# A three-mixer trunk on one core: the scan's decay work ordered behind its group's values, group sums in four column tiles, running sums by zero-padded products

## The chip, the cores and the metric

The kernel runs on one core of a Trainium2 chip. The metric is the device time of one execution in microseconds (us), and lower is better. Three timed runs of the kernel before gave 811.83, 812.42 and 811.11 us, median 811.83. The profile is that of a further execution, which took 812.16 us.

Engine names in the profile: PE is TensorE's matrix products and PEld its weight loads; DVE is VectorE, ACT is ScalarE, POOL is GpSimd, SP is SyncE. A name with q (ACTq) is an engine's queue issuing a DMA. L829 is line 829 of the kernel before.

## What is computed

Two residual layers on 256 tokens of 1024 channels, and a final norm. In each layer one wide projection of the normalised stream feeds three causal mixers (a state-space scan in the Mamba-2 manner, sliding-window attention, forgetting attention). Each mixer's output is projected back, weighted by a sigmoid gate, and the sum goes through an output projection. Cut to what the change touches:

```python
def ssd_chunked_scan(xh, dt, a, bm, cm):        # chunks of 128 tokens, 4 groups of 4 heads
    x_dt = x * dtc[..., None]
    a_cum = jnp.cumsum(dtc * a, axis=-1)          # running sum inside a chunk
    seg = a_cum[..., :, None] - a_cum[..., None, :]
    decay = jnp.where(causal, jnp.exp(jnp.where(causal, seg, 0.0)), 0.0)
    y_diag = einsum(cb[:, :, None] * decay, x_dt)
    decay_states = jnp.exp(a_cum[..., -1:] - a_cum)
    states = einsum(bc, decay_states, x_dt)
    ...
def grouped_rms_norm(y, w, groups):               # 4 groups of 256 channels
    y = y * rsqrt(mean(y * y over the group) + EPS)
    ...
def forgetting_attention_branch(...):
    cum = cumsum(log_sigmoid(f_logit + f_bias))   # over all 256 tokens
    scores + cum[query] - cum[key], causal softmax, times values
```

## The kernel before

**Weights and products.** Weights stream through `raw` tiles by SyncE's DMAs. ScalarE rounds each to a high half `hi` (L293), VectorE takes the low half `lo` as the difference (L294), and TensorE multiplies with both (fast float32r products, the records `mm<-hi`, `mm<-lo`). The activations are split in the same way. Small products (scores, values, transposes, the ones here) are plain float32 and write to PSUM tiles `mx`.

**Order of the work.** TensorE's order is written out by a planner while the program is built. `clock["t"]` counts the planned TensorE time (`mm` and `transpose`, L103 to L113, add a cost each). The dense products run in a fixed list. Every side job is a generator that yields a delay; `pump()` and `drain()` place its next stage between dense products when the planned clock has passed that delay. On TensorE that order is kept. On VectorE, ScalarE and GpSimd the scheduler of the tile framework picks an order that it deems ready first, and the built program then issues each engine's instructions strictly in that order. `tc.issue_after(x)` orders what is issued in its block behind `x`. `T("L1", ...)` takes a tile from a rotating set of buffers of that size.

**The decay logits** (`decay_logits`, L765 to L811). VectorE computes the steps `dt` and the log forget values `lf` for both chunks of 128 tokens, and writes `rates` (tokens on partitions; chunk, kind, 16 heads). After `D_CUM` TensorE makes the running sums: `tri` times the scan's rates gives tokens by heads (L799, kept as `acum`); `rates` as weights against `tri` give heads by tokens, 32 rows for each chunk (L801); a third product with `ones` adds the first chunk's total to the second chunk's forget sums (L803). ScalarE copies the 64 rows out and writes them to `cumd` in DRAM (L807 to L811), so that they can be read back by DMA as broadcasts over all partitions.

**The scan** (`ssd_group`, L852 to L915; four groups in each layer). A group fetches its broadcast `bcg` from `cumd` (L858, issued by ScalarE's queue), yields, transposes its inputs on TensorE (L867) and evicts them times `dt` into `xdt` (L868, VectorE). Then come `ds` (last running sum less the token's own, 128x4, L871), its exponential (L872, ScalarE), `xds = xdt * ds` (L874), eight subtractions with the causal mask (L881), the exponentials of the two decays (L883) and of `cross` (L887). A stage later two products C times B are made (L893, L894) and multiplied into the decays (L896), and a stage after that TensorE makes the outputs (L901 to L910) and VectorE adds the skip term (L913).

**Others in the same stretch.** The convolution of the scan's inputs runs three taps on VectorE (L829), a tanh on ScalarE (L835) and a product on VectorE (L836). Sliding-window attention transposes its probabilities on TensorE; ScalarE copies the first half (L676), VectorE masks the second half with `other` (L678) and with `tri` (L679); the products with values of two quads of heads follow (L711, the batches `mx<-L,bias` and `mm<-L,bias`). Forgetting attention loads a bias per pair of heads (L1050), masks it on GpSimd (L1057) and uses it on VectorE (L649).

**Group norm of the scan's output** (`group_norms`, L959 to L978). For each of four groups and each half of the tokens, the 128x128 tile of squares is the weights and two columns of `ones` are the moving operand (L966): the sums land with tokens on partitions. VectorE scales (L968), GpSimd raises to the power -1/2 (L969), VectorE makes one Newton step (L973 to L975). `u_proj_normed` uses the roots at its evictions (L1000, L1002).

Of the kernel before, what the change touches and what calls it, by code (L numbers as in the profile page):

```python
# [13 lines left out]
AF = mybir.ActivationFunctionType  # L14
ALU = mybir.AluOpType

P = 128
S = 256
# [4 lines left out]
EPS = 1e-6  # L23

D_SOFT, D_SOFT2, D_EVAC, D_SSD, D_SSD2 = 7.0, 3.0, 3.0, 8.0, 4.0
D_K, D_Q, D_QK, D_G0, D_FOX, D_BDMA, D_BIAS, D_BC, D_SSD3 = 6.0, 5.5, 2.0, 8.0, 0.0, 4.0, 2.6, 5.5, 1.0
D_GN1, D_GN2, D_CUM, D_H, D_M = 8.0, 13.5, 17.0, (4.8, 6.4), 5.0
BUDGET = 1.35
T_PP, T_SSD, T_BIAS = 1, 1, 1
D_MEET = 12.0  # L30
# [20 lines left out]
def hybrid_trunk(  # L51
# [5 lines left out]
    nc = tc.nc  # L57
# [45 lines left out]
    def mm(o, a, b, **kw):  # L103
        n = b.free_size()
        if a.dtype == F32R:
            clock["t"] += max(0.094, n / 2350.0)
        else:
            clock["t"] += max(0.2, n / 587.0) * (0.5 if a.free_size() == 64 or a.shape[0] == 32 else 1.0)
        nc.tensor.matmul(o, a, b, **kw)  # L109

    def transpose(o, a, i):
        clock["t"] += 0.109
        nc.tensor.transpose(o, a, i)  # L113
# [76 lines left out]
    ident = T("ident", [P, P])  # L190
    make_identity(nc, ident)
    tri = T("tri", [P, P])
# [3 lines left out]
    negtri = T("negtri", [P, P])  # L196
# [7 lines left out]
    ones = onesr.bitcast(F32)  # L204
# [223 lines left out]
    for l in range(L):  # L428
        y = Layer()
# [335 lines left out]
    def decay_logits(y):  # L765
        u = y.u

        tmp = T("L1", [P, 4, 2, 32])
        e = w = tmp[:, 0, :, :]
        act(e, u, AF.Abs)  # L770
        act(e, e, AF.Exp, scale=-1.0)
        s = tmp[:, 1, :, :]
        ts(s, e, 2.0, None, op0=ALU.add)
        nc.vector.reciprocal(s, s)
        tt(s, s, e, op=ALU.mult)
        s2 = tmp[:, 2, :, :]
        tt(s2, s, s, op=ALU.mult)
        q = tmp[:, 3, :, :].rearrange("p t c -> p (t c)")
        s2f = s2.rearrange("p t c -> p (t c)")
        sf = s.rearrange("p t c -> p (t c)")  # L780
        ts(q, s2f, 1.0 / 19.0, None, op0=ALU.mult)
        for m in (17, 15, 13, 11, 9, 7, 5, 3):
            stt(q, q, 1.0 / m, s2f, op0=ALU.add, op1=ALU.mult)
        stt(q, q, 1.0, sf, op0=ALU.add, op1=ALU.mult)
        q3 = q.rearrange("p (t c) -> p t c", t=2)
        y.dt = T("dt", [P, 2, 16])
        rates = T("rates", [P, 2, 2, 16])
        lf = tmp[:, 2, :, 0:16]
        ts(w[:, :, 0:16], u[:, :, 0:16], 0.0, 0.5, op0=ALU.max, op1=ALU.mult)
        tt(y.dt, w[:, :, 0:16], q3[:, :, 0:16], op=ALU.add)  # L790
        ts(y.dt, y.dt, 2.0, None, op0=ALU.mult)
        ts(w[:, :, 16:32], u[:, :, 16:32], 0.0, 0.5, op0=ALU.min, op1=ALU.mult)
        tt(lf, w[:, :, 16:32], q3[:, :, 16:32], op=ALU.subtract)
        ts(rates[:, :, 0, :], lf, -16.0, None, op0=ALU.mult)
        tt(rates[:, :, 1, :], y.dt, bc(y.nega, 1, 2), op=ALU.mult)
        yield D_CUM

        pc = pmx()
        mm(pc[:, P:P + 32], tri, rates[:, :, 1, :], start=True, stop=True)  # L799
        for c in range(2):  # L800
            mm(pc[32 - 32 * c:64 - 32 * c, 0:P], rates[:, c, :, :].rearrange("p w c -> p (w c)"), tri,  # L801
               start=True, stop=(c == 0))
        mm(pc[0:16, 0:P], rates[:, 0, 0, :], ones, start=False, stop=True)  # L803
        y.acum = T("acum", [P, 2, 16])
        act(y.acum, pc[:, P:P + 32].rearrange("p (t c) -> p t c", t=2), AF.Copy)
        cum = T("L1", [64, P])
        act(cum, pc[0:64, 0:P], AF.Copy)  # L807
        y.cumd = dr.tile([2, 16, S], F32, name=f"cumd{y.l}", tag=f"cumd{y.l}")
        for c in range(2):
            nc.scalar.dma_start(y.cumd[:, :, c * P:(c + 1) * P].rearrange("w c s -> (w c) s"),  # L810
                                cum[32 - 32 * c:64 - 32 * c, :])  # L811


    def u_conv(y, u, c):
# [37 lines left out]
    def ssd_group(y, g):  # L852
        yield lambda: not any(m[2] == 1 for m in waiting)
        if g == 0:
            yield D_SCAN
        yield "bcg"
        bcg = T("L4", [P, 4, S])
        nc.scalar.dma_start(bcg, y.cumd[1, 4 * g:4 * g + 4, :].partition_broadcast(P))  # L858
        yield D_BC
        yield "ssd"  # L860
        xdt = T("L2", [P, 2, 256])
        hs = slice(4 * g, 4 * g + 4)
        p = pmx()
        for t in range(2):
            for j in range(2):
                n = 2 * t + j
                transpose(p[:, n * P:(n + 1) * P], y.xs[:, 2 * g + j, t * P:(t + 1) * P], ident)  # L867
        tt(xdt.rearrange("p t (h d) -> p t h d", h=4), p.rearrange("p (t h d) -> p t h d", t=2, h=4),  # L868
           bc(y.dt[:, :, hs], 3, 64), op=ALU.mult)
        ds = T("ds", [P, 4], bufs=2)  # L870
        tt(ds, bcg[:, :, P - 1], y.acum[:, 0, hs], op=ALU.subtract)  # L871
        act(ds, ds, AF.Exp)  # L872
        xds = T("L1", [P, 256])
        tt(xds.rearrange("p (h d) -> p h d", h=4), xdt[:, 0, :].rearrange("p (h d) -> p h d", h=4),  # L874
           bc(ds, 2, 64), op=ALU.mult)
        decs = []
        for c in range(2):
            tk = slice(c * P, (c + 1) * P)
            dec = T("L2", [P, 4, P])
            for h in range(4):  # L880
                stt(dec[:, h, :], bcg[:, h, tk], y.acum[:, c, 4 * g + h:4 * g + h + 1], negtri,  # L881
                    op0=ALU.subtract, op1=ALU.add)
            act(dec, dec, AF.Exp)  # L883
            decs.append(dec)

        cross = T("L2", [P, 4, P])
        act(cross, bcg[:, :, P:S], AF.Exp)  # L887
        decs.append(cross)
        yield D_SSD
        tokens["bcg"] += 1  # L890

        p = pmx()
        mm(p[:, 0:S], y.bcT[:, g, 0:P], y.bcT[:, 4 + g, :], start=True, stop=True)  # L893
        mm(p[:, S:3 * P], y.bcT[:, g, P:S], y.bcT[:, 4 + g, P:S], start=True, stop=True)  # L894
        for dec, c in zip(decs, (0, 2, 1)):
            tt(dec, dec, bc(p[:, c * P:(c + 1) * P], 1, 4), op=ALU.mult)  # L896
# [62 lines left out]
    def group_norms(y, squares):  # L959


        p = pmx()
        for g, q in enumerate(squares):
            for t in range(2):
                c = 4 * g + 2 * t
                mm(p[:, c:c + 2], q[:, t * P:(t + 1) * P], ones[:, 0:2], start=True, stop=True)  # L966
        v, r0 = T("sm", [P, 8]), T("sm", [P, 8])
        ts(v, p[:, 0:16].rearrange("p (g i) -> p g i", i=2)[:, :, 0], 1.0 / 256, 4 * EPS, op0=ALU.mult, op1=ALU.add)  # L968
        gtt(r0, v, mhalf, op=ALU.pow)  # L969

        def newton():
            y.roots = T("rs", [P, 8], bufs=4)
            tt(v, r0, v, op=ALU.mult)  # L973
# [431 lines left out]
    with tc.manual_schedule(engines={ENG.PE, ENG.DVE, ENG.Activation, ENG.Pool}):  # L1405
# [11 lines left out]
        p = pmx()  # L1417
# [151 lines left out]
```

## Time and profile before

| what | us |
|---|---|
| median of three timed runs | 811.83 |
| the profiled execution | 812.16 |
| its span in the trace | 810.5 |
| PE busy, all | 799.6 |
| PE busy between 100 and 200 us | 98.63 |
| PE busy between 500 and 600 us | 98.49 |
| DVE busy between 200 and 300 us | 93.08 |

The times on the left of timelines and chain pieces are us from the start of the span. Layer 1 fills about the first half of it and layer 2 the second, with the same stages about 398 us later. "Busy" of PE is the union of its product records. A product in float32 shows as two records, a fast one or a transpose as one. A bracket at the end of a timeline row says how long the engine had been idle and what released it. In a row of a group the numbers after the bar are the total busy time and the mean ns of one record.

### The profile page before, as it was taken

To read this page: it belongs to the slowest core of one execution; us is meant where nothing else is said; L and a number is where in the kernel's file an instruction comes from. 1 tells how busy PE (TensorE), PEld (TensorE's weight loads), DVE (VectorE), ACT (ScalarE), POOL (GpSimd) and SP (SyncE) were. 2 spreads that over 40 slices of the span, in tenths; PEclk is the share of its full clock that TensorE was granted. 3 is DMA by queue.
4 is the path that set the end of the run, shared out by engine and by line. 5 is a ranking of instruction groups with operands and counts; after the bars stand their busy time and mean duration, and the time that the engine had idled before them with its cause. 6 is when DMAs were issued, how large, how long until landed. Compare 5 with 4: busy or idle time off the path is not lost.

```text
span 810.5 us, 14858 instructions
## 1 busy us (share of the span) xinstructions
PE 799.6 (99%) x5178; PEld 714.4 (88%) x5178; DVE 684.6 (84%) x1412; ACT 532.7 (66%) x1142; POOL 167.8 (21%) x236
## 2 busy tenths in 40 slices
PE   9999999999999999999999999999999999999996
PEld 8998988888888888888999899887889988888896
DVE  6878999898898998795785889998979999869865
ACT  7777768775775785543665588676747768745452
POOL 3066113130321000033001831122312110002000
PEclk9999999999999999999999999999999999999999
DMA  9997887697665565676678987679986646567632
GB/s 314 277 265 178 245 228 202 185 291 230 174 210 159 165 189 179 211 248 209 221 249 259 247 204 213 153 216 257 280 226 185 201 143 186 175 226 218 211 107 75
DMA packets 138826, 170.43 MB, mean 210 GB/s; under 512 B 9352, under 2 KB 106464, under 8 KB 138752
## 3 DMA queue, kind: packets, MB, share of 16 engines
q1 hardware_dynamic: 114960, 140.53, 55.1%
q0 software_dynamic: 13328, 13.29, 10.2%
q10 hardware_dynamic: 10464, 15.67, 6.4%
q8 instruction: 41, 0.67, 0.3%
q14 instruction: 33, 0.27, 0.1%
HBM read 154.71 MB, written 2.16 MB: 194 GB/s over the span
## 4 chain that ended last, share of the span: by engine, by line
PE 97%; DMA 1%; DVE 1%; ACT 0%; issue 0%; POOL 0%; ACTq 0%; POOLq 0%
PE mm L109 83%; PE mx L109 10%; PE mx L113 4%; DMA L<-cumd 1%; DVE lo L294 0%; DVE L L678 0%; ACT L L293 0%; DVE L L836 0%; DVE L L1431 0%; DVE L L1088 0%; ACT L L1435 0%; ACT L L1212 0%; DVE L L829 0%; DVE L L1187 0%; DVE L L1191 0%
## 5 line engine op out<-in xcount | busy, mean ns | idle before, releaser
L109 PE MATMUL mm<-L,hi 128*128 128x512 f32 x1056 | 354.0, 387 | 0.2
L294 DVE TENSOR_TENSOR lo<-raw,hi 128x1024 fp32r<-128x1024 f32 (+1 forms) x276 | 313.1, 1154 | 38.8 <-ACT hi L293 36.0
L109 PE MATMUL mm<-hi,L 128*128 128x512 f32 (+2 forms) x1168 | 303.1, 349 | 0.1
L293 ACT ACTIVATE hi<-raw 128x1024 fp32r<-128x1024 f32 (+1 forms) x276 | 266.1, 983 | 55.9 <-PE mm L109 49.0
L109 PE MATMUL mm<-L,lo 128*128 128x256 f32 x1056 | 266.6, 273 | 0.0
L109 PEld LDWEIGHTS mm<-hi,L 128*128 128x128 f32 x1168 | 205.9, 190 | 22.4 <-issue 1.0
L109 PEld LDWEIGHTS mm<-L,hi 128*128 128x128 f32 x1056 | 194.9, 190 | 27.2 <-issue 5.4
L109 PEld LDWEIGHTS mm<-L,lo 128*128 128x128 f32 x1056 | 202.1, 191 | 5.4
L109 PE MATMUL mm<-lo,L 128*128 128x512 f32 (+2 forms) x584 | 201.5, 347 | 0.0
L109 PEld LDWEIGHTS mm<-lo,L 128*128 128x128 f32 x584 | 110.2, 190 | 10.8 <-DVE lo L294 0.2
L491 POOL DMA_DIRECT2D L<-L x68 | 59.5, 895 | 194.0 <-ACT L L490 131.2
L829 DVE SCALAR_TENSOR_TENSOR L<-L,vec,L 128x255 f32<-128x255 f32 (+2 forms) x96 | 46.3, 482 | 1.8
L1057 POOL TENSOR_SCALAR_AFFINE_SELECT bias<-bias 128x128 f32<-128x128 f32 x64 | 32.1, 535 | 74.7 <-DMA bias<-cumd 70.9
L489 ACT ACTIVATE L<-mm 128x256 f32<-128x256 f32 x84 | 31.9, 380 | 19.5 <-PE mm L109 15.5
L655 ACT ACTIVATE pp<-pp,nm 128x128 f32<-128x128 f32 x64 | 28.2, 442 | 23.8 <-DVE nm L649 23.8
L1091 ACT ACTIVATE L<-L 128x512 f32<-128x512 f32 x24 | 15.1, 631 | 39.3 <-DVE L L1088 34.7
L491 POOL DMA_DIRECT2D qt<-L x16 | 13.8, 859 | 78.7 <-ACT qt L490 71.8
L1088 DVE TENSOR_TENSOR L<-mm,L 128x512 f32<-128x512 f32 x22 | 15.1, 688 | 16.5 <-PE mm L109 8.8
L613 ACT ACTIVATE pp<-pp,nm 128x128 f32<-128x128 f32 x32 | 12.6, 394 | 24.7 <-DVE nm L618 23.9
L835 ACT ACTIVATE L<-L 128x256 f32<-128x256 f32 x32 | 13.4, 418 | 22.2 <-DVE L L829 22.1
L490 ACT ACTIVATE L<-mm 128x256 f32<-128x256 f32 x68 | 26.2, 385 | 1.8 <-DMA L<-L 1.8
L1124 POOL TENSOR_TENSOR L<-L,L 128x512 f32<-128x512 f32 x8 | 11.9, 1491 | 71.3 <-DVE L L1123 69.9
(211 smaller groups left out, 920.0 us busy)
## 6 DMA issues: line engine op xcount, KB each, us to landing
raw<-in_w_in_dram SPq DMA_DIRECT2D x191, 512.0 KB, 5.0
raw<-in_w_proj_dram SPq DMA_DIRECT2D x48, 512.0 KB, 6.1
L<-L POOLq DMA_DIRECT2D x72, 128.0 KB, 5.3
raw<-in_w_out_dram SPq DMA_DIRECT2D x16, 512.0 KB, 5.6
bias<-cumd ACTq DMA_DIRECT2D x16, 256.0 KB, 3.5
L<-cumd ACTq DMA_DIRECT2D x8, 512.0 KB, 7.0
L<-in_gate_bias_dram ACTq DMA_DIRECT2D x12, 256.0 KB, 5.9
qt<-L POOLq DMA_DIRECT2D x16, 128.0 KB, 5.9
```

The source lines that it names most:

```text
L109: nc.tensor.matmul(o, a, b, **kw)
L113: nc.tensor.transpose(o, a, i)
L293: keep(act)(hi, src, AF.Copy)
L294: keep(tt)(lo, src, hi.bitcast(F32), op=ALU.subtract)
L489: act(halves(lo), ordered(p[:, S:2 * S]), AF.Copy)
L490: last = act(halves(out), ordered(p[:, 0:S]), AF.Copy)
L491: nc.gpsimd.dma_start(out, lo, accum_op=ALU.add)
L655: act(pp[:, i, sl], pp[:, i, sl], AF.Exp, scale=-1.0, bias=nm[:, e:e + 1], accum_out=sums[:, e:e + 1])
L829: stt(a[:, s:S], x_[:, 0:S - s], y.vec[:, 16 * j + u:16 * j + u + 1], a[:, s:S], op0=ALU.mult, op1=ALU.add)
L1057: nc.gpsimd.affine_select(out=bias[:, i, dst], in_=bias[:, i, src], compare_op=ALU.is_ge, fill=NEG, base=0, pattern=[[-1, P]], channel_mul ...
L1088: tt(halves(g), p, halves(y.gb), op=ALU.add)
L1091: finish(act(g, g, AF.Tanh, scale=0.5))
```

## The change

Three edits, and a constant that goes with the second (`D_GN2`, which the kernel before defines and doesn't use).

1. In `ssd_group` the `ds` work, `xds` and the decays are built inside `tc.issue_after(own.ins)`, where `own` is the eviction into `xdt`; `cross` is built behind the exponential of the second decay.
2. In `group_norms` the roles of weights and moving operand are exchanged: 32 columns of `ones` are the weights, a group's 128x256 squares move, and group g writes PSUM rows 32g to 32g+31 (each of these rows holds the same sums). ScalarE copies the 128x256 sums out, after `D_GN2` = 3.0 of planned time TensorE transposes them in two halves, and VectorE picks one column of 32 from each group.
3. In `decay_logits` the rates are written into the first columns of a zeroed 128x128 tile `all_`, and the first chunk's forget rates once more into a zeroed tile `past`, at the columns of the second chunk's forget rates. Two products of full width, accumulated, give all 64 rows; the order of the two chunks' rows is exchanged. GpSimd zeroes both tiles by one memset.

```diff
-D_GN1, D_GN2, D_CUM, D_H, D_M = 8.0, 13.5, 17.0, (4.8, 6.4), 5.0
+D_GN1, D_GN2, D_CUM, D_H, D_M = 8.0, 3.0, 17.0, (4.8, 6.4), 5.0
...
-        rates = T("rates", [P, 2, 2, 16])
+        wide = T("L1", [P, 2, P])
+        nc.gpsimd.memset(wide, 0.0)
+        all_, past = wide[:, 0, :], wide[:, 1, :]
+        rates = all_[:, 0:64].rearrange("p (t w c) -> p t w c", t=2, w=2)
...
+        ts(past[:, 32:48], lf[:, 0, :], -16.0, None, op0=ALU.mult)
         yield D_CUM
 
         pc = pmx()
+        mm(pc[:, 0:P], all_, tri, start=True, stop=False)
+        mm(pc[:, 0:P], past, ones, start=False, stop=True)
         mm(pc[:, P:P + 32], tri, rates[:, :, 1, :], start=True, stop=True)
-        for c in range(2):
-            mm(pc[32 - 32 * c:64 - 32 * c, 0:P], rates[:, c, :, :].rearrange("p w c -> p (w c)"), tri,
-               start=True, stop=(c == 0))
-        mm(pc[0:16, 0:P], rates[:, 0, 0, :], ones, start=False, stop=True)
...
-                                cum[32 - 32 * c:64 - 32 * c, :])
+                                cum[32 * c:32 + 32 * c, :])
...
-        tt(xdt.rearrange("p t (h d) -> p t h d", h=4), p.rearrange("p (t h d) -> p t h d", t=2, h=4),
-           bc(y.dt[:, :, hs], 3, 64), op=ALU.mult)
-        ds = T("ds", [P, 4], bufs=2)
-        tt(ds, bcg[:, :, P - 1], y.acum[:, 0, hs], op=ALU.subtract)
-        act(ds, ds, AF.Exp)
+        own = tt(xdt.rearrange("p t (h d) -> p t h d", h=4), p.rearrange("p (t h d) -> p t h d", t=2, h=4),
+                 bc(y.dt[:, :, hs], 3, 64), op=ALU.mult)
         xds = T("L1", [P, 256])
-        tt(xds.rearrange("p (h d) -> p h d", h=4), xdt[:, 0, :].rearrange("p (h d) -> p h d", h=4),
-           bc(ds, 2, 64), op=ALU.mult)
         decs = []
-        for c in range(2):
...
+        with tc.issue_after(own.ins):
+            ds = T("ds", [P, 4], bufs=2)
+            tt(ds, bcg[:, :, P - 1], y.acum[:, 0, hs], op=ALU.subtract)
+            act(ds, ds, AF.Exp)
+            tt(xds.rearrange("p (h d) -> p h d", h=4), xdt[:, 0, :].rearrange("p (h d) -> p h d", h=4),
+               bc(ds, 2, 64), op=ALU.mult)
+            for c in range(2):
...
+                grown = act(dec, dec, AF.Exp)
+                decs.append(dec)
 
         cross = T("L2", [P, 4, P])
-        act(cross, bcg[:, :, P:S], AF.Exp)
+        with tc.issue_after(grown.ins):
+            act(cross, bcg[:, :, P:S], AF.Exp)
...
         for g, q in enumerate(squares):
-            for t in range(2):
-                c = 4 * g + 2 * t
-                mm(p[:, c:c + 2], q[:, t * P:(t + 1) * P], ones[:, 0:2], start=True, stop=True)
+            mm(p[32 * g:32 * g + 32, 0:S], ones[:, 0:32], q, start=True, stop=True)
+        r = T("L1", [P, S])
+        act(r, p[:, 0:S], AF.Copy)
+        yield D_GN2
+        p = pmx()
+        for t in range(2):
+            transpose(p[:, t * P:(t + 1) * P], r[:, t * P:(t + 1) * P], ident)
         v, r0 = T("sm", [P, 8]), T("sm", [P, 8])
-        ts(v, p[:, 0:16].rearrange("p (g i) -> p g i", i=2)[:, :, 0], 1.0 / 256, 4 * EPS, op0=ALU.mult, op1=ALU.add)
+        ts(v.rearrange("p (g t) -> p t g", t=2), p[:, 0:S].rearrange("p (t g i) -> p t g i", t=2, i=32)[:, :, :, 0],
+           1.0 / 256, 4 * EPS, op0=ALU.mult, op1=ALU.add)
```

More of the change, by code (lines that the diff above doesn't have):

```diff
@@ L867, in ssd_group @@
                 transpose(p[:, n * P:(n + 1) * P], y.xs[:, 2 * g + j, t * P:(t + 1) * P], ident)
-        tt(xdt.rearrange("p t (h d) -> p t h d", h=4), p.rearrange("p (t h d) -> p t h d", t=2, h=4),
-           bc(y.dt[:, :, hs], 3, 64), op=ALU.mult)
-        ds = T("ds", [P, 4], bufs=2)
-        tt(ds, bcg[:, :, P - 1], y.acum[:, 0, hs], op=ALU.subtract)
-        act(ds, ds, AF.Exp)
+        own = tt(xdt.rearrange("p t (h d) -> p t h d", h=4), p.rearrange("p (t h d) -> p t h d", t=2, h=4),
+                 bc(y.dt[:, :, hs], 3, 64), op=ALU.mult)
         xds = T("L1", [P, 256])
-        tt(xds.rearrange("p (h d) -> p h d", h=4), xdt[:, 0, :].rearrange("p (h d) -> p h d", h=4),
-           bc(ds, 2, 64), op=ALU.mult)
         decs = []
-        for c in range(2):
[L878 to L884, printed above, removed]
+        with tc.issue_after(own.ins):
[5 more added lines that the diff above has]
+            for c in range(2):
+                tk = slice(c * P, (c + 1) * P)
+                dec = T("L2", [P, 4, P])
+                for h in range(4):
+                    stt(dec[:, h, :], bcg[:, h, tk], y.acum[:, c, 4 * g + h:4 * g + h + 1], negtri,
+                        op0=ALU.subtract, op1=ALU.add)
+                grown = act(dec, dec, AF.Exp)
+                decs.append(dec)
         cross = T("L2", [P, 4, P])
-        act(cross, bcg[:, :, P:S], AF.Exp)
+        with tc.issue_after(grown.ins):
+            act(cross, bcg[:, :, P:S], AF.Exp)
         decs.append(cross)
```

## The prediction

> **What bounds the kernel now.** I read the busy shares of the page first, then the chain that ended last, then the windows, then PE's waits, then the timelines at those places.
>
> ```profile
> PE 799.6 (99%) x5178; PEld 714.4 (88%) x5178; DVE 684.6 (84%) x1412; ACT 532.7 (66%) x1142; POOL 167.8 (21%) x236
> ...
> PE 97%; DMA 1%; DVE 1%; ACT 0%; issue 0%; POOL 0%; ACTq 0%; POOLq 0%
> ```
>
> ```profile
> 100.00:200.00 100.00, 98.63 (x638) 86.48 (x637) 91.21 (x198) 71.42 (x160) 20.76 (x28) 1.00 0.81 227
> 200.00:300.00 100.00, 100.00 (x743) 89.13 (x742) 93.08 (x247) 73.39 (x178) 15.79 (x28) 1.00 0.62 184
> ...
> 500.00:600.00 100.00, 98.49 (x637) 86.36 (x636) 90.82 (x196) 69.59 (x158) 21.87 (x29) 1.00 0.82 229
> ```
>
> ```profile
> PE mm L109 <- DVE L L678: 2.7, 2, 1.5
> ```
>
> The windows give a stretch, its length, then the busy time of PE, PEld, DVE, ACT and POOL, the clock, the DMA share and GB/s; the waits give the total in us, how often, and the longest. PE is the bound: 97% of the chain, and 100 of 100 us between 200 and 300. So time is won or lost in two ways only: by work on PE, and by idle PE. The idle is 1.37 us between 100 and 200 and 1.51 between 500 and 600, and nearly all of it is one event, once per layer: PE waits for L678, which masks the transposed probabilities for the second product with values. Three timelines show it (start, length, engine, line, operation, tiles, count, idle before and its releaser), of VectorE, ACT and PE:
>
> ```profile
> 154.25 1.00 DVE L829 SCALAR_TENSOR_TENSOR L<-L,vec,L 128x255 f32<-128x255 f32 x2
> 157.97 0.17 DVE L871 TENSOR_TENSOR ds<-L,acum 128x4 f32<-128x4 f32 x1 [2.72 <-DMA L<-cumd]
> ...
> 158.45 2.35 DVE L294 TENSOR_TENSOR lo<-raw,hi 128x1024 fp32r<-128x1024 f32 x2
> 160.72 0.42 DVE L836 SCALAR_TENSOR_TENSOR L<-L,L 128x256 f32<-128x256 f32 x1
> 161.05 0.68 DVE L678 TENSOR_TENSOR L<-mx,other 128x512 f32<-128x512 f32 x1
> ...
> 555.65 0.16 DVE L871 TENSOR_TENSOR ds<-L,acum 128x4 f32<-128x4 f32 x1 [2.94 <-DMA L<-cumd]
> ```
>
> ```profile
> 154.65 2.00 ACT L293 ACTIVATE hi<-raw 128x1024 fp32r<-128x1024 f32 x2
> 158.62 0.42 ACT L835 ACTIVATE L<-L 128x256 f32<-128x256 f32 x1 [1.98 <-DVE L L829]
> ```
>
> ```profile
> 159.12 1.52 PE L109 MATMUL mx<-L,bias 128*64 128x256 f32 x16
> 161.88 1.60 PE L109 MATMUL mm<-L,bias 128*64 128x256 f32 x16 [1.24 <-DVE L L678]
> ...
> 559.57 1.60 PE L109 MATMUL mm<-L,bias 128*64 128x256 f32 x16 [1.47 <-DVE L L678]
> ```
>
> The scan's first `ds` (L871) stands in VectorE's order between the conv taps, long before its group is wanted, and its operand comes by a DMA that has not landed. VectorE stands still for 2.72 us; all that is behind it in its order (the third tap, two splits, L836, L678) is that much later, and PE is out of work for 1.24 us. In layer 2 it is 2.94 us, then 1.47.
>
> **The change part by part.**
>
> *The decay work behind its group's values.* `ds`, its exponential, `xds` and the decays of all eight groups are ordered behind the eviction into `xdt` (L868). In the order in which the built kernel issues on VectorE each `ds` does come behind its own L868, for the first group some 28 us later than now, with its DMA long landed; SP's order is as before. What is late next? Without the halt the third tap runs at 155.2. The two splits follow ACT's halves (154.65 + 2.00) and end near 158.0; L835 runs at 156.6, L836 at 158.0, L678 from 158.4 to 159.1. PE needs it when its first batch ends, 159.12 + 1.52 = 160.6. That is 1.5 us to spare, so I take the whole wait away: 1.24 + 1.47 = **2.71 us**. Bounds: 0, if another wait takes its place, and the whole idle of the two windows, 2.88.
>
> What the moved instructions meet where they now stand, in order of time on ACT, VectorE, the queues and POOL, and last the price of the exponential:
>
> ```profile
> 184.37 1.06 ACT L293 ACTIVATE hi<-raw 128x1024 fp32r<-128x1024 f32 x1 [0.24 <-PE mm L109]
> ...
> 185.30 0.68 DVE L868 TENSOR_TENSOR L<-mx,dt 128x512 f32<-128x512 f32 x1
> ...
> 196.15 1.88 DVE L896 TENSOR_TENSOR L<-L,mx 128x512 f32<-128x512 f32 x3
> ...
> 234.10 1.30 ACTq L1050 DMA_DIRECT2D bias<-cumd  x1
> ...
> 235.58 0.69 DVE L868 TENSOR_TENSOR L<-mx,dt 128x512 f32<-128x512 f32 x1
> ...
> 238.89 3.49 POOL L1057 TENSOR_SCALAR_AFFINE_SELECT bias<-bias 128x128 f32<-128x128 f32 x4 [0.89 <-DMA bias<-cumd]
> ...
> 254.10 0.29 DVE L649 CUSTOM_DVE_ANT_0 pp<-mx,bias 128x128 f32<-128x128 f32 x1 [0.26 <-PE mx L109]
> ...
> L872 ACT ACTIVATE ds<-ds x8: 199/206/211, 160.5 to 641.0; 128x4 f32<-128x4 f32 x8
> ```
>
> Behind L868 VectorE now does `ds`, two to six other operations, and then `xds`, which needs the exponential (0.21 us). ACT is free at 185.4, before `ds` is done at about 186.1, so `xds` waits 0 to 0.2 us. The decays are wanted at 196.15 and are ready some seven us before. In ACT's order the exponential also stands ahead of the second bias DMA in the third and fourth groups: that DMA goes out behind a `ds` at about 236.7 instead of at 234.10. Its masks on POOL then end near 245 instead of 242.4, and L649 wants them from 254.10 on. So I cost the move at nothing.
>
> *Group sums.* Five pieces of the chain (start, length, what, count), then forms of the batches at 65.67 and 159.12, then PE's timeline:
>
> ```profile
> 65.67 1.52 PE mx L109 x32
> ...
> 77.87 0.44 PE mx L113 x4
> ...
> 221.20 0.65 PE mx L109 x4
> ...
> 314.25 1.68 PE mx L109 x16
> ...
> 711.93 1.68 PE mx L109 x16
> ```
>
> ```profile
> L109 PE MATMUL mx<-L,qt 32*128 32x256 f32 x16 | 1.0, 375 | 0.0
> ```
>
> ```profile
> L109 PE MATMUL mx<-L,bias x16: 272/326/430, 159.1 to 160.4; 128*64 128x256 f32 x8, 128*64 128x128 f32 x8
> ```
>
> ```profile
> 158.48 0.38 PE L109 MATMUL mm<-L,hi 128*128 128x512 f32 x1
> ...
> 158.81 0.38 PE L109 MATMUL mm<-L,hi 128*128 128x512 f32 x1
> ```
>
> Eight products per layer go; a product in float32 is two records, so 16 records and 1.68 us. Four come, with 32 columns of ones as weights and 256 moving columns: 8 records, or 16 units, a unit being a record of 128 moving columns. The trace has no such product; three rows price a unit. Over the whole array (221.20, the two products of L893 and L894: 6 units in 0.65) it is 0.108, and 16 are 1.73 us. Two tiles of 64 columns side by side (8 records of 256 and 8 of 128, 24 units in the 1.52 at 159.12): 0.063, and 16 are 1.01. Four tiles of 32 rows (65.67: 16 records of 256, the other 16 of 128, 48 units in 1.52): 0.032, and 16 are 0.51. The new products are four tiles of 32 too, so that row is the nearest, and I take 0.51. Add 0.1 for changing the shape: from 158.48 to 158.81 a product of 512 columns and one of 256 take 0.33, so the one of 512 takes 0.22; the one at 158.81 should be followed at 159.03, and the tiled batch starts at 159.12. Two transposes are half of 0.44. Gain: 1.68 - 0.51 - 0.10 - 0.22 = 0.85 per layer, **1.70 us**. Bounds per layer: 0.35 in pairs, a loss of 0.27 one after another (1.68 - 1.73 - 0.22).
>
> Between sums and transposes comes an ACT copy of 128x256. What it meets, on ACT and VectorE:
>
> ```profile
> 315.70 0.63 ACT L1091 ACTIVATE L<-L 128x512 f32<-128x512 f32 x1 [4.77 <-DVE L L1088]
> ...
> 317.93 0.17 DVE L973 TENSOR_TENSOR sm<-sm,sm 128x8 f32<-128x8 f32 x1 [1.80 <-POOL sm L969]
> ...
> 333.01 0.67 ACT L1000 ACTIVATE L<-mm,rs 128x512 f32<-128x512 f32 x1
> ...
> 713.26 0.63 ACT L1091 ACTIVATE L<-L 128x512 f32<-128x512 f32 x1 [3.70 <-DVE L L1088]
> ```
>
> In the built order the copy is right ahead of L1091, so in ACT's idle 4.77 and 3.70 us, and the transposes come 24 products of 512 columns behind the sums, 24 x 0.22 = 5.2 us. PE doesn't wait for it; without that cover it would, for what is left of the copy. POOL's power, for which VectorE waited until 317.93, comes some six us later, so the roots are there near 324.5. Their first use is at 333.01.
>
> *Running sums and the memset.* A piece of the chain (layer 1; I take layer 2 as the same), and POOL's timeline:
>
> ```profile
> 117.89 0.70 PE mx L109 x8
> ```
>
> ```profile
> 105.37 0.86 POOL L491 DMA_DIRECT2D L<-L  x1 [5.85 <-ACT L L835]
> ```
>
> Eight records, six of them narrow, become six of full width: 0.66 at the transposes' 0.11 each, and no change of shape. I take 0.1 per layer, **0.20 us**; bounds 0 and 0.25 each. The memset stands in POOL's idle 5.85 us, and VectorE's one extra operation of 16 columns delays nothing that PE needs then.
>
> **Sum.** 2.71 + 1.70 + 0.20 = 4.61 us. The profiled execution took 812.16 (span 810.5), which becomes 807.55; the median of the runs shown, 811.83, is 0.33 lower: **807.2 us**.
>
> **Rivals.**
>
> *Column tiles one after another.* The four tiles share all 128 rows, and no row here has four of them at once. The sums would then cost 0.27 a layer more than before, and the gain is 2.71 - 0.54 + 0.20 = 2.37: 809.5. Against it: pairs of 64 columns run at 0.063 a unit, not 0.108. The Trainium skill has a rule that would have it so (TensorE: Matmul & The Clock Gate, Part 3: Packing small matmuls — row/col tiling): a weight load overlaps products in flight only where the row group differs. By that rule the pairs at 159.12 would not overlap either, and there the trace disagrees with it. Chance 0.10.
>
> *The wait has a successor.* L678 is late all the same, because both splits and L836 ahead of it wait for ACT. That leaves 1.90: 809.9. For it: these three do wait for ACT here. Against: the 1.5 us to spare. Chance 0.13.
>
> *Slower: VectorE held in the round trip to ACT.* In the eight groups `xds` waits for an exponential that ACT reaches only behind two weight splits of 1.06. That is 2.1, less some 0.6 of decays between: 1.5 us a group, 12 in all, in stretches where VectorE is up to 93% busy. If all of it reached PE: 811.8 - 4.6 + 12 = 819. It decides from 0.8 us a group that reach PE (6.2 in all). Against: ACT is free at 185.4, and seven us lie between decays and use. Chance 0.05.
>
> *It doesn't do what it says.* The order excludes that for `ds`; 0.02 for anything of the kind.
>
> **How the numbers follow.** The forecast has 0.70. A measurement can tell about 0.2%, 1.6 us, from no change, so faster means below 810.2. The forecast, nearly all of the first rival and most of the second are faster: 0.87; same 0.08; slower 0.05. The forecast alone, by the bounds of its terms and the spread of the runs (811.11 to 812.42), is 806.0 to 809.2. To leave out no more than 2 in 10 it reaches to both rivals: 805.8 to 810.0.
>
> **What would show it.** `ds` doesn't wait for its DMA, PE doesn't wait for L678, and both windows show PE at nearly 100. The group sums are 8 records in about 0.5 us per layer (1.0 or 1.7 speak for the rival), and PE doesn't wait for the copy. VectorE has no idle ahead of `xds`. I am wrong if PE shows a new wait of over 1 us near 160 or 320 or in the scan.

## The result, and the profile after

The changed kernel takes 808.50 us in the median of its first runs, beside 811.42 for the kernel before on the same chip: a ratio of 0.9957, with a 95% interval of 0.9945 to 0.9970. Timed again beside other kernels it took 808.10, ratio 0.9952 (0.9939 to 0.9964). Of 811.9 us that is 3.5 to 3.9 us less. The prediction was 807.2, in a range of 805.8 to 810.0.

The page of the changed kernel first, with the busy times, and then PE's waits, which give the total in us, how often and the longest:

```profile
PE 796.9 (99%) x5162; PEld 710.7 (88%) x5162; DVE 684.6 (85%) x1414; ACT 534.0 (66%) x1144; POOL 171.6 (21%) x238
```

```profile
PE mx L113 <- POOL ident masks.py:199: 1.5, 1, 1.5
PE mx L109 <- ACT hi L1453: 0.8, 2, 0.4
PE mm L109 <- DVE L L1097: 0.7, 2, 0.4
```

L678 is no longer in the list, which now has these three rows: the first stands in the kernel before too, the second belongs to the start, the third is new to the list and comes up again below. The two windows that held PE's idle time (stretch, length, busy time of PE, PEld, DVE, ACT and POOL, clock, DMA share, GB/s):

```profile
100.00:200.00 100.00, 99.57 (x645) 87.71 (x643) 92.52 (x198) 71.68 (x161) 21.40 (x29) 1.00 0.83 230
...
500.00:600.00 100.00, 99.74 (x645) 87.86 (x644) 91.05 (x194) 70.51 (x159) 23.33 (x30) 1.00 0.83 234
```

PE's idle time there falls from 1.37 and 1.51 us to 0.43 and 0.26. VectorE's timeline at the place where `ds` had stood, and PE's:

```profile
154.98 1.52 DVE L831 SCALAR_TENSOR_TENSOR L<-L,vec,L 128x255 f32<-128x255 f32 x3
...
159.07 0.68 DVE L678 TENSOR_TENSOR L<-mx,other 128x512 f32<-128x512 f32 x1
```

```profile
159.85 1.52 PE L109 MATMUL mx<-L,bias 128*64 128x256 f32 x16
161.20 1.47 PE L109 MATMUL mm<-L,bias 128*64 128x256 f32 x16
...
555.15 1.52 PE L109 MATMUL mx<-L,bias 128*64 128x256 f32 x16
556.50 1.47 PE L109 MATMUL mm<-L,bias 128*64 128x256 f32 x16
```

The three taps are one row now, with no idle bracket, and L678 ends at 159.75, 1.6 us before PE's first batch does. The second batch starts 1.35 us behind the start of the first, where it had been 2.76 (161.88 - 159.12) and 3.00. That is 1.41 and 1.65 us, more than the 1.24 and 1.47 that the waits view gave for the same two places: a batch that doesn't wait also starts 0.17 us ahead of the modelled end of the one before it. The batch itself is 0.13 shorter as well (1.47, and 1.60 in the kernel before), so the products behind it gain 1.54 and 1.77, as the table below has it.

The group sums on PE in the kernel before:

```profile
313.22 0.38 PE L109 MATMUL mm<-lo,L 128*128 128x512 f32 x1
...
313.87 0.38 PE L109 MATMUL mm<-lo,L 128*128 128x512 f32 x1
314.09 1.84 PE L109 MATMUL mx<-ones,L 128*128 128x2 f32 x16
...
316.31 0.38 PE L109 MATMUL mm<-lo,L 128*128 128x512 f32 x1
```

The same in the changed kernel, with the transposes, and their copy on ACT:

```profile
313.06 0.38 PE L109 MATMUL mm<-lo,L 128*128 128x512 f32 x1
313.37 0.64 PE L109 MATMUL mx<-L,ones 128*32 128x256 f32 x8
313.94 0.70 PE L109 MATMUL mm<-hi,L 128*128 128x512 f32 x2
314.47 0.38 PE L109 MATMUL mm<-lo,L 128*128 128x512 f32 x1
...
319.00 0.38 PE L109 MATMUL mm<-lo,L 128*128 128x512 f32 x1
319.22 0.38 PE L113 MATMUL mx<-ident,L 128*128 128x128 f32 x2
...
319.87 0.38 PE L109 MATMUL mm<-lo,L 128*128 128x512 f32 x1
```

```profile
314.12 0.38 ACT L970 ACTIVATE L<-mx 128x256 f32<-128x256 f32 x1 [4.01 <-PE mx L109]
```

From one product with `lo` to the next it is 0.65 us without anything between (313.22 to 313.87 in the kernel before). With the old sums between it was 2.44, with the new sums it is 1.41, with the two transposes 0.87. So the sums cost 0.76 where they had cost 1.79, and the transposes 0.22. The eight records take 0.57 from the first start to the next product. PE waits neither for the copy nor later for the roots.

Two kernels whose products stand in the same order can be compared product by product. The table takes the start of each PE record in the trace after less that of its partner before, and lists where this difference moves, in us:

| at (time before) | step | what stands there |
|---|---|---|
| 5 to 9 | +0.48 | first weights |
| 118, 516 | -0.25, -0.23 | running sums |
| 124, 521 | +0.20, +0.21 | transposes of the probabilities |
| 150, 548 | +0.30, +0.21 | gate products |
| 161, 559 | -1.54, -1.77 | L678 |
| 315, 713 | -1.04, -1.02 | group sums |
| 321, 719 | +0.24, +0.22 | their transposes |
| sum | -3.99 | spans 810.5 and 806.4 |

The third and the fourth row are losses that the prediction did not have. The start differs from execution to execution, as the second traces below show.

### The profile page after: what moved, and what is told of

The parts are those of the page before. It is cut to its first block, busy times and chain, and to the rows that moved or that the text cites. A ratio compares the mean times of both kernels' runs of the same rounds, so it can differ in the third digit from the quotient of the medians.

```text
span 806.4 us, 14834 instructions
## 1 busy us (share of the span) xinstructions
PE 796.9 (99%) x5162; PEld 710.7 (88%) x5162; DVE 684.6 (85%) x1414; ACT 534.0 (66%) x1144; POOL 171.6 (21%) x238
## 4 chain that ended last, share of the span: by engine, by line
PE 97%; DVE 1%; DMA 1%; issue 0%; ACT 0%; SPq 0%; DVEq 0%
PE mm L109 84%; PE mx L109 10%; PE mx L113 3%; DMA raw<-in_w_in_dram 1%; DVE lo L294 0%; DVE L L1097 0%; SPq L363 0%; SPq L189 0%; DVE L L1440 0%; ACT L L1444 0%; ACT hi L1453 0%; ACT L L1221 0%; DVE L L1196 0%; DVE L L1200 0%; DVE L L288 0%
## 5 line engine op out<-in xcount | busy, mean ns | idle before, releaser
L978 POOL TENSOR_TENSOR sm<-sm,mhalf 128x8 f32<-128x8 f32 x2 | 5.2, 2593 | 111.6 <-DVE sm L976 111.6
L1097 DVE TENSOR_TENSOR L<-mm,L 128x512 f32<-128x512 f32 x22 | 15.1, 686 | 13.6 <-PE mm L109 12.1
```

The lines of the kernel that those rows point to most:

```text
L1097: tt(halves(g), p, halves(y.gb), op=ALU.add)
```

## The experiments

Each kernel was timed beside the kernel before on its chip; the last has one execution only:

| kernel | median us | ratio to before (95%) |
|---|---|---|
| e0_before_again | 812.24 | 1.0007 (0.9999 to 1.0016) |
| e1_scan_only | 809.38 | 0.9970 (0.9959 to 0.9981) |
| e2_sums_only | 810.14 | 0.9981 (0.9972 to 0.9990) |
| e3_running_only | 812.32 | 1.0009 (1.0001 to 1.0018) |
| e4_scan_and_sums | 807.93 | 0.9949 (0.9935 to 0.9962) |
| e7_own_buffer | 807.89 | 0.9947 (0.9934 to 0.9959) |
| e9_both | 807.54 | 0.9944 (0.9932 to 0.9957) |
| e12_after_again | 808.10 | 0.9952 (0.9939 to 0.9964) |
| e10_best | 807.20 | 0.9942 (0.9929 to 0.9954) |
| e11_more_dve | 808.82 | 0.9961 (0.9947 to 0.9974) |
| e6_no_cover | 809.09 | 0.9964 (0.9951 to 0.9976) |
| e5_wider_tiles | 810.16, once | |

The kernels were timed in three groups: the first four; e4, e7, e9 and e5; the rest. The medians of before in these groups were 811.92, 812.13 and 811.89. Intervals of 0.2 to 0.3% do not part kernels that lie 0.5 us apart; for those the traces are paired, one execution of each kernel. Two traces of the same changed kernel (after and e12_after_again) differ by 0.11 us at one place and by 0.16 over all that follows the start, so a total of less than some 0.2 us is not told apart by pairing either.

**The kernel before once more.** No edit.

> The kernel before, unchanged, for a second trace of it: how far the start (the weights that land first) and the two halts at the decay work differ between executions. My theory: the halts of VectorE differ by less than 0.3 us and the start by up to 0.5 us. Rival: the halts differ by 0.5 us or more each, since they end with the landing of a transfer, and that is why the medians differ by 2.9 us and the two profiled executions by 4.0.

PE's waits for L678 and VectorE's for the transfer, in the second trace of before:

```profile
PE mm L109 <- DVE L L678: 1.9, 2, 0.9
```

```profile
DVE ds L871 <- DMA L<-cumd: 4.8, 2, 2.4
```

They were 2.7 and 5.7 in the first one. PE was 0.86 us later behind the start, 0.51 later behind the first halt and 0.02 behind the second, and both traces end at 810.5. The halts moved by 0.32 and 0.53, and PE's waits by 0.31 and 0.54, so in the size of the halts the rival came nearer; but they did not make these two executions differ in time. The halts took up lateness that arose ahead of them: the transfer was issued 0.83 and 0.56 us later than in the first trace, and `ds` behind its landing started 0.52 and 0.03 later. That is not the whole of it, since in the trace of e2_sums_only the transfer of layer 1 was issued 0.21 later and `ds` started 0.22 earlier. From issue to `ds` it was 6.7 to 7.6 us in four traces (before, e0, e2, e3); what sets it stays open. What the halt is worth depends on the execution.

**The scan's order alone.** To the kernel before are added only the two lines `with tc.issue_after(own.ins):` and `with tc.issue_after(grown.ins):` with their blocks:

```diff
-        tt(xdt..., p..., bc(y.dt[:, :, hs], 3, 64), op=ALU.mult)
+        own = tt(xdt..., p..., bc(y.dt[:, :, hs], 3, 64), op=ALU.mult)
...
+        with tc.issue_after(own.ins):
             ds = T("ds", [P, 4], bufs=2)
...
+        with tc.issue_after(grown.ins):
+            act(cross, bcg[:, :, P:S], AF.Exp)
```

> The kernel before with only the decay work issued behind its group's values; group sums and running sums as before. My theory: this part removes the two waits of PE for L678, and set against the trace of before PE is 1.5 us earlier behind the first and 1.8 behind the second, so the time is 3.0 to 3.3 us below the kernel before, near 808.2, and PE shows no wait for L678. Rival: the profiled execution of before had longer halts than the median one, and most of the change's gain is that of the group sums; then it is only 1.0 to 1.5 us below the kernel before, near 810.2.

Measured: 0.9970, 2.4 us below (1.5 to 3.3), between the two. PE doesn't wait for L678. Paired with the first trace of before, PE gains 1.54 at 161 and 1.77 at 559, 3.3 together; paired with the second one 1.22 and 1.23, so 2.4. The mechanism is shown, and its size is that of the halts in the execution it is set against.

**The group sums alone.** With `D_GN2` = 3.0, and VectorE's pick of the columns as in the change:

```diff
-            for t in range(2):
-                c = 4 * g + 2 * t
-                mm(p[:, c:c + 2], q[:, t * P:(t + 1) * P], ones[:, 0:2], start=True, stop=True)
+            mm(p[32 * g:32 * g + 32, 0:S], ones[:, 0:32], q, start=True, stop=True)
+        r = T("L1", [P, S])
+        act(r, p[:, 0:S], AF.Copy)
+        yield D_GN2
+        p = pmx()
+        for t in range(2):
+            transpose(p[:, t * P:(t + 1) * P], r[:, t * P:(t + 1) * P], ident)
```

> The kernel before with only the group sums in four column tiles, their copy and transposes. My theory: 0.80 us per layer (the batch 1.04 shorter, the transposes 0.24), so 1.6 us below the kernel before, near 809.8, with both waits for L678 as they were. Rival: part of the gain is lost in the product with the output weights, because the roots come some six us later; then less than 1.0 us below, and PE shows a wait near 335 or 730 us.

Measured: 0.9981, 1.5 us below (0.8 to 2.3). In its trace PE gains 1.04 at 315 and loses 0.24 at 321, the same again in layer 2, and has no wait near 335 or 730. The theory holds for the sums. The waits for L678 were not as they had been: 1.3 us in all where the first trace of before has 2.7, and the one of layer 1 stands ahead of everything that this edit touches, so it differs by the execution.

**The running sums alone.** The lines of the diff in `decay_logits`, and nothing else:

```diff
-        rates = T("rates", [P, 2, 2, 16])
+        wide = T("L1", [P, 2, P])
+        nc.gpsimd.memset(wide, 0.0)
...
+        ts(past[:, 32:48], lf[:, 0, :], -16.0, None, op0=ALU.mult)
...
+        mm(pc[:, 0:P], all_, tri, start=True, stop=False)
+        mm(pc[:, 0:P], past, ones, start=False, stop=True)
```

> The kernel before with only the running sums by zero-padded products, the memset and the one more operation on VectorE. My theory: the batch is 0.23 us shorter per layer, but six us later PE waits for L642 on VectorE, which is 0.08 later for the operation more, so nothing is left: within 0.2 us of the kernel before, and in the trace PE is 0.2 us earlier behind the batch and not earlier behind the transposes of the probabilities. Rival: the late VectorE in the trace of the changed kernel came from the slower start of that one execution; then the 0.23 us stay, 0.4 to 0.5 below the kernel before.

Measured: 1.0009 (1.0001 to 1.0018): nothing is won, and 0.1 to 1.5 us are lost, where the theory had at most 0.2. The rival falls. The batch and the transposes behind it, on PE in the kernel before and in the changed one (after):

```profile
117.51 0.38 PE L109 MATMUL mm<-L,hi 128*128 128x512 f32 x1
117.73 0.30 PE L109 MATMUL mx<-rates,tri 128*128 128x32 f32 x2
...
118.52 0.48 PE L109 MATMUL mm<-L,hi 128*128 128x512 f32 x1
...
123.65 0.38 PE L109 MATMUL mm<-L,hi 128*128 128x512 f32 x1
123.87 0.60 PE L113 MATMUL mx<-ident,pp 128*128 128x128 f32 x4
```

```profile
117.97 0.38 PE L109 MATMUL mm<-L,hi 128*128 128x512 f32 x1
118.18 0.38 PE L109 MATMUL mx<-tri,L 128*128 128x128 f32 x2
...
118.77 0.46 PE L109 MATMUL mm<-L,hi 128*128 128x512 f32 x1
...
123.88 0.38 PE L109 MATMUL mm<-L,hi 128*128 128x512 f32 x1
124.27 0.63 PE L113 MATMUL mx<-ident,pp 128*128 128x128 f32 x4
```

From the product ahead of the batch to the one behind it took 1.01 us before (117.51 to 118.52) and takes 0.80. But the transposes of `pp` come 0.39 us behind the product ahead of them, where it had been 0.22: they wait, too shortly for the list of waits. What they wait for is the first L642 on VectorE, which divides the probabilities by their sums, before and after:

```profile
122.88 0.69 DVE L642 TENSOR_TENSOR pp<-pp,rsum 128x512 f32<-128x512 f32 x1
```

```profile
123.43 0.69 DVE L642 TENSOR_TENSOR pp<-pp,rsum 128x512 f32<-128x512 f32 x1
```

It ended 0.30 us ahead of the transposes before, and ends 0.15 ahead of them now. That gap is 0.15 in after, e3, e7, e11 and e12 alike, while the product ahead of them moves: there the transposes follow VectorE and not PE. Between 100 and 124 us no idle time of VectorE is listed in before, e3 or after; so the one operation of 16 columns more (L799, 0.09 from its start to the next) is 0.09 at L642, and what PE wins by the shorter batch it waits for here, down to the 0.15.

```profile
116.25 0.17 DVE L799 TENSOR_SCALAR L<-L 128x16 f32<-128x16 f32 x1
116.33 0.48 DVE L831 SCALAR_TENSOR_TENSOR L<-L,vec,L 128x254 f32<-128x254 f32 x1
```

Behind that, in the trace of after and of e3, a tanh on ACT starts later behind its wait. ACT's rows of it, for before, after, e7_own_buffer and e9_both:

```profile
137.26 0.42 ACT L835 ACTIVATE L<-L 128x256 f32<-128x256 f32 x1 [0.60 <-DVE L L829]
```

```profile
137.99 0.42 ACT L837 ACTIVATE L<-L 128x256 f32<-128x256 f32 x1 [0.88 <-DVE L L831]
```

```profile
138.07 0.42 ACT L837 ACTIVATE L<-L 128x256 f32<-128x256 f32 x1 [0.60 <-DVE L L831]
```

```profile
138.11 0.42 ACT L837 ACTIVATE L<-L 128x256 f32<-128x256 f32 x1 [0.88 <-DVE L L831]
```

VectorE carries the 0.28 on, and at the gate's eviction (L1097) it is PE that waits. In layer 2 the tanh near 533 us starts without this delay in all four, so there the loss at the gate is VectorE's own lateness.

**The running sums taken back.** The changed kernel with the diff above undone.

> The changed kernel with the running sums of before (four products, no memset, no operation more on VectorE). My theory: the running sums cost more than they give, since PE then waits for VectorE near 124, 150, 521 and 548 us; without them the time is 0.3 to 0.8 us below the changed kernel, and PE is not later behind 150 than behind 130. Rival: the running-sum part measured alone was slower by chance; then this kernel is 0 to 0.5 us above the changed kernel.

Measured: 0.9949, and paired with the first trace of after PE ends 0.61 earlier, 0.49 of it behind the start. At 151 and 548 it is 0.30 and 0.24 better, at 124 and 521 0.18 and 0.21, and the batches cost 0.21 and 0.23. VectorE's start times, set against this kernel's, show the added operation itself: in after VectorE is 0.12 later ahead of it and 0.22 behind it in layer 1, 0.40 and 0.50 in layer 2, and keeps that lateness through both L642. The theory holds: without the running sums the change is better, by 0.49 us in the traces.

**A buffer of its own.**

```diff
-        wide = T("L1", [P, 2, P])
+        wide = T("wide", [P, 2, P])
```

> The changed kernel, the zero-padded tile of the running sums in a buffer of its own instead of one of the ring L1. My theory: the tile shifts the ring by one buffer, and the tanh at L837 near 137 us then writes a buffer that a transfer still reads: it starts 0.28 us late, VectorE and PE behind it. With an own buffer that delay is gone, and PE loses 0.1 us or less at 150 instead of 0.3; the time is 0.2 to 0.3 us below the changed kernel. Rival: the delay has nothing to do with the buffer; then L837 starts at the same 0.28 us late, and the time is the same within 0.1 us.

Measured: the delay is gone (0.60, third row above), and PE ends 0.24 us earlier behind an equal start, 0.17 of it at 151; the times (0.9947 beside 0.9952 of e12_after_again) do not resolve that. As predicted, but the reason given is not shown, as the next kernel tells.

**Three small operations on ACT.** On top of the own buffer:

```diff
-        ts(q, s2f, 1.0 / 19.0, None, op0=ALU.mult)
+        act(q, s2f, AF.Copy, scale=1.0 / 19.0)
...
-        ts(rates[:, :, 0, :], lf, -16.0, None, op0=ALU.mult)
+        act(rates[:, :, 0, :], lf, AF.Copy, scale=-16.0)
...
-        ts(past[:, 32:48], lf[:, 0, :], -16.0, None, op0=ALU.mult)
+        act(past[:, 32:48], lf[:, 0, :], AF.Copy, scale=-16.0)
```

> The changed kernel with the own buffer and with three small operations of the logits' decay (the polynomial's first scaling, the two scalings by -16) on ACT instead of VectorE. My theory: between 100 and 150 us VectorE is gapless and PE waits for it by 0.2 us at the transposes of the probabilities and by some 0.4 us at the gate's eviction, in each layer, so each 0.1 us less on VectorE is 0.1 us less of time until these waits are gone: three operations at 0.09 us each give 0.27 per layer, with the buffer some 0.6 to 0.8 us below the changed kernel. Rival: PE is the bound there and VectorE's time is worth nothing; then within 0.2 us of the kernel with the own buffer alone.

Measured: 0.9944; PE ends 0.49 us earlier than in after behind an equal start, a little less than the 0.6 to 0.8 expected, and 0.25 earlier than with the buffer alone. At 124 and 521 it wins the 0.20 back, so less work on VectorE there is time won on PE. But the 0.88 is there again, though the buffer is its own and the built order has no wait for a transfer at L837. The theory of the buffer falls. What goes with the delay in every trace is the place of L837 in ACT's stream: where it is three instructions further on than in before (after, e3, e5, e6, e9, e11, e12) it starts 0.34 us behind the record of its wait, else 0.06 (before, e0, e1, e2, e4, e7, and e10, where it is two further on). Why that is stays open.

**Wider tiles.**

```diff
-            mm(p[32 * g:32 * g + 32, 0:S], ones[:, 0:32], q, start=True, stop=True)
+            if y.l == 0:
+                mm(p[64 * (g % 2):64 * (g % 2) + 64, 0:S], ones[:, 0:64], q, start=(g < 2), stop=(g > 1))
+            else:
+                mm(p[:, 0:S], ones, q, start=(g == 0), stop=(g == 3))
```

> The changed kernel with the group sums in two tiles of 64 columns in the first layer and over all 128 columns in the second; the groups' sums run together in both, so the values are not the reference's, and the number of records, their moving columns and what follows are the same. My theory: tiles in different columns run side by side and a tile of 32 has a quarter of the price: 0.5 us in the changed kernel, 1.0 in the first layer here, 1.7 in the second. Rival: the records of four tiles take as long as any other, one after another, and the 0.64 us of the changed kernel is a matter of how ends are modelled; then PE is behind all three forms of the batch at the same time.

PE in layer 1 (two tiles of 64 columns) and in layer 2 (all columns):

```profile
313.84 1.08 PE L109 MATMUL mx<-L,ones 128*64 128x256 f32 x8
314.85 0.70 PE L109 MATMUL mm<-hi,L 128*128 128x512 f32 x2
```

```profile
709.60 1.89 PE L109 MATMUL mx<-L,ones 128*128 128x256 f32 x8
711.14 0.78 PE L109 MATMUL mm<-hi,L 128*128 128x512 f32 x2
```

From the first start to the next product: 0.57 with four tiles, 1.01 with two, 1.54 with one. Set against after, PE is 0.45 us later behind the batch in layer 1 and 0.96 in layer 2. So the shortness is PE's own time and no matter of modelled ends. The rival falls. In these two forms the groups also accumulate in the same rows, which the four tiles don't; but products over the whole array that do not accumulate were no faster (0.108 us a unit at L893 and L894 of the kernel before, 1.73 for 16). All four tiles share the 128 rows, and they overlap; the rule of the Trainium skill that the prediction weighed (TensorE: Matmul & The Clock Gate, Part 3: Packing small matmuls — row/col tiling: a weight load overlaps products in flight only where the row group differs) doesn't agree with these three numbers.

**The changed kernel once more.** No edit.

> The changed kernel, unchanged, for a second trace and for its time beside the kernels of this call. My theory: its three repeating losses are there again (0.2 us at the transposes of the probabilities near 124 us, a gap of 0.8 us in the products near 151 us where the kernel before has 0.5, and the tanh near 137 us that starts 0.34 us behind its wait), and only the start differs; the time is 3.3 to 4.0 us below the kernel before. Rival: these losses were those of one execution and do not come again.

Measured: 808.10. Its start was 0.41 us earlier than in the first trace of after; the waits at 124 and 151 and the 0.88 at L837 are there again. At 124 PE followed the product ahead by 0.41, and at 151 it lost 0.11, where VectorE set the pace: so of an early start part is lost again.

**Without the cover.** The line `yield D_GN2` is taken out, so the transposes follow the sums at once.

> The changed kernel with the transposes of the group sums right behind the sums, without the 24 products between. My theory: PE waits for the copy on ACT (0.38 us), and for what ACT has ahead of it, 0.6 to 1.0 us per layer: 1.2 to 2.0 us above the changed kernel. Rival: ACT is so quick that the copy is hidden in the batch's own end; then less than 0.4 us above it.

```profile
313.14 0.64 PE L109 MATMUL mx<-L,ones 128*32 128x256 f32 x8
314.34 0.44 PE L113 MATMUL mx<-ident,L 128*128 128x128 f32 x2 [0.56 <-ACT L L970]
314.53 0.68 PE L109 MATMUL mm<-hi,L 128*128 128x512 f32 x2
```

Measured: 1.0 us above the changed kernel timed beside it (809.09 and 808.10), just under what was expected, and 0.6 per layer in the pairing, the lower end of it. The 24 products hide that much.

**More work on VectorE.**

```diff
-        tt(s, s, e, op=ALU.mult)
+        step_ = tt(s, s, e, op=ALU.mult)
+        junk = T("junk", [P, P])
+        with tc.issue_after(step_.ins):
+            for _ in range(4):
+                ts(junk, ident, 1.0, None, op0=ALU.mult)
```

> The changed kernel with four more operations of 128x128 on VectorE per layer, in the logits' decay near 107 us, that compute nothing which is used: some 0.8 us more of VectorE's time, PE's order unchanged. My theory: VectorE is the bound between 100 and 150 us, and PE waits for it at 124 and 150 us; so 0.6 to 0.8 us per layer come out, 1.2 to 1.6 us in all above the changed kernel. Rival: PE is the bound and VectorE has slack; then 0 to 0.3 us above it.

Measured: 0.7 us above the changed kernel timed beside it (808.82 and 808.10), between the two. The size was wrong and the mechanism right. The logits' chain is of small operations that need each other's result: in after two of them with nothing between start 0.24 and 0.27 us apart (L783 at 113.54, 113.78, and L784 at 114.05). With one of the four between, each starts some 0.13 behind the one ahead. So the four take part of the time in which VectorE waits for itself, and at the split ahead of the softmax (118 us) VectorE is only 0.24 later than in after, behind an equal start. That 0.24 comes out on PE in full:

```profile
123.75 0.38 PE L109 MATMUL mm<-L,hi 128*128 128x512 f32 x1
124.40 0.63 PE L113 MATMUL mx<-ident,pp 128*128 128x128 f32 x4 [0.27 <-DVE sums L639]
```

The transposes are 0.65 behind the product ahead, and not 0.39; paired with after PE loses 0.25 at 124 and 0.27 by 520.

**The best version.** The scan's order, the column tiles, the running sums of before, and two of the small operations on ACT (the first two edits of e9_both).

> The scan's order and the column tiles of the changed kernel, the running sums of before, and two small operations of the logits' decay (the polynomial's first scaling, the scaling by -16) on ACT instead of VectorE. My theory: VectorE is late by 0.28 us near 150 us even in the kernel before, and 0.2 us less on it per layer is worth 0.1 to 0.2 per layer: 0.2 to 0.4 us below the kernel with the running sums of before, some 0.7 below the changed kernel. Rival: nothing waits there any more or ACT becomes late instead; then it is the same as the kernel with the running sums of before, 0.5 us below the changed kernel.

Measured: 807.20, ratio 0.9942 (0.9929 to 0.9954), 0.9 us below the changed kernel timed beside it. Behind an equal start PE ends 0.83 earlier than in after, 0.34 more than e4_scan_and_sums does, as the theory had it. The gate products near 151, in the kernel before (first fence), in after (second) and here:

```profile
150.15 0.96 PE L109 MATMUL mm<-L,hi 128*128 128x512 f32 x2
150.94 0.38 PE L109 MATMUL mm<-L,lo 128*128 128x256 f32 x2
```

```profile
150.58 0.38 PE L109 MATMUL mm<-L,hi 128*128 128x512 f32 x1
151.38 0.45 PE L109 MATMUL mm<-L,hi 128*128 128x512 f32 x1 [0.42 <-DVE L L1097]
151.67 0.38 PE L109 MATMUL mm<-L,lo 128*128 128x256 f32 x2
```

```profile
150.10 0.79 PE L109 MATMUL mm<-L,hi 128*128 128x512 f32 x2
150.73 0.38 PE L109 MATMUL mm<-L,lo 128*128 128x256 f32 x2
```

From the product with `hi` to the pair with `lo` it is 0.79, 1.09 and 0.63 us. In the kernel before the list of waits shows nothing here, since the wait hides in a row of two records that lasts 0.96.

## Why the prediction was right, and where it was not

- *The wait for L678 goes whole* (2.71): right in the mechanism. The halt is gone, the spare time was 1.6 us where 1.5 had been worked out, and no successor appears there. Alone it is worth 2.4 us (1.5 to 3.3). That the size came so near is partly luck, since two errors work against each other: the waits view shows less than PE gains at these places (2.7 against 3.3 with the first trace of before, 1.9 against 2.4 with the second), and it was read from the execution with the longest waits. They were 1.9 us in the second trace of before, 2.4 in that of e3 and 1.3 in that of e2.
- *The moved work costs nothing*: right. In the trace of after VectorE has no idle ahead of `xds`; ACT waits for `ds` in two of eight groups, 1.3 us in all, with no wait of PE in the list behind it. The slower rival did not come.
- *Group sums* (1.70): right, 1.60 in the traces, 1.5 in the times. The four tiles took 0.57 and the changes of shape some 0.1 on either side, 0.76 where 0.61 had been said; but the old sums had cost 1.79 where 1.68 had been said (2.44 from 313.87 to 316.31, less the 0.65). The transposes cost 0.22, and the copy is covered.
- *Running sums* (0.20): wrong. The batch was worth more than said (0.23 per layer, the upper bound was 0.25), and yet the part cost 0.5 us. The step that failed is "VectorE's one extra operation of 16 columns delays nothing that PE needs then". PE needed the softmax six us later, VectorE had no idle time before it, and only 0.30 us lay between the two, of which 0.15 could be used up. The shorter batch (0.23) and the later VectorE (0.09) were more than that, so PE waited at 124 and 521, and for the lateness of VectorE again at 151 and 548. Some 0.17 of the loss at 151 goes with the late tanh, whose cause stays open. A PE that is 99% busy was read as PE alone being the bound.
- *The sum*: 4.61 forecast, 3.5 and 3.9 measured. Of what is missing the running sums make 0.7 (0.20 and 0.49) and the group sums 0.1. The 0.3 between 2.71 and 2.4 lies within the interval of e1_scan_only and is not resolved. The time stayed in the range, with one part of three wrong in its sign. That e10_best measures the forecast time, 807.20, is chance: it leaves the running sums out and moves two operations that the forecast did not count.

## What to carry to other kernels

A list of waits with a threshold shows the large ones only: where a PE row spans more time than its records, or starts later behind the one ahead than its neighbours do, another engine may set the pace, and what is added to that engine there comes out on PE (0.24 us on VectorE came out as 0.25 in e11_more_dve). A halt that ends with a landing is worth what the execution at hand makes of it; a second trace of the same kernel shows how much that varies, before a gain is worked out from it. Cover for a short round trip (here 24 products for one copy, 0.6 us a layer) is cheap and worth its line.

## What the runs showed of the hardware

- Four products of 32 weight columns each over the same 128 rows run side by side: eight records of 256 columns in 0.57 us, against 1.01 in two tiles and 1.54 untiled.
- Independent operations put between dependent ones on VectorE cost less than their length: four of 128x128, 0.22 us each in the trace, made VectorE 0.24 us later.
- One activation on ACT (the tanh near 137 us) starts 0.34 us behind the record of its wait in seven traces and 0.06 in seven others. The delay goes with three more instructions ahead of it in ACT's stream. No run settles why.
